# Straight programs, an identity from VectorE and a different row order for m tile 0 in a tuned matmul-subtract kernel

## The chip, the cores and the metric

One core of one Trainium2 chip. The metric is the device time of one execution in microseconds (us), without a profiler; the span that a profile gives is some 2 us shorter (209.0 for a run of 211.0). Where two kernels are compared, they ran in the same rounds on the same chip; a ratio is the mean time of one kernel's fast runs over the mean of the other's of the same rounds, so it is not quite the ratio of the medians that stand beside it.

## The reference

```python
batch, m, k, n = 16, 512, 1024, 768
x         = randn(batch, m, k)   # float32
weight    = randn(k, n)          # float32
sub_value = randn(batch, m, n)   # float32
out       = np.matmul(x, weight) - sub_value      # float32
```

That is 8192 rows, worked on as 64 m tiles of 128 rows. Loads are 62 MB, stores 25 MB.

## The kernel before

Every engine has its own list of instructions, emitted once all lists are complete. SyncE issues 38 large transfers in a fixed order ('x' and 's' are loads, 'o' stores; the numbers are the first m tile and how many):

```python
TRANSFERS = [
    ('x', 0, 1), ('w', 0, 1), ('x', 1, 1), ('w', 1, 1), ('x', 2, 1), ('w', 2, 1),
    ('x', 3, 2), ('w', 3, 1), ('s', 0, 1), ('x', 5, 3), ('s', 1, 3), ('x', 8, 4),
    ('s', 4, 4), ('x', 12, 4), ('s', 8, 8), ('x', 16, 2), ...
    ('x', 24, 8), ('o', 0, 8), ('s', 24, 8), ... ('o', 56, 5), ('o', 61, 2), ('o', 63, 1),
]
```

A run of eight m tiles is a block of 1024 rows in which partition p holds rows 8p to 8p+7, so a transfer of one m tile reads rows that lie eight apart. ScalarE casts x to 16 bits. For most tiles TensorE transposes against an identity matrix that GpSimd makes; for one pair of tiles in three, VectorE transposes (pieces of 32x256 in the trace, 435 ns each). TensorE multiplies, VectorE subtracts. TensorE's program is a straight part and a loop of ten rounds, six tiles each; at the very start it runs matmuls on zeros ("idle") until the first tile is there.

At the start three engines go around their whole program once: in a first turn they branch past it, in a second one they run it.

```python
    turn = nc.alloc_registers("turn", engines=engines)      # PE, DVE, Activation
    nc.regs_mov(turn, 0)
    with nc.body("turn_head", valid_engines=engines):
        nc.br_cmp(turn, 0, on_true="past", on_false="work", comp_op="IS_EQ", engines=engines)
    with nc.body("work", valid_engines=engines):
        act.emit(act.ops)
        dve.emit(dve.ops[:NEAR])          # NEAR = 140
        ...                               # pe: straight part, loop, rest
    with nc.body("past", valid_engines=engines):
        nc.regs_alu(turn, turn, 1, op=mybir.AluOpType.add)
        nc.br_cmp(turn, 2, on_true="turn_head", on_false="rest", comp_op="IS_LT", engines=engines)
    nc.switch_bb("rest")
    dve.emit(dve.ops[NEAR:])
```

## Time and profile before

| | before |
|---|---|
| time, median of 3 runs | 210.98 us (210.87 to 211.11) |
| span of the profile | 209.0 us |
| TensorE busy | 196.5 us, 94% |
| share of the 16 DMA engines' time | 97.7% |
| bytes moved | 87.08 MB |
| first x tile usable | 6.0 us |
| stretch in which TensorE never waits | 45.79 us to its end |
| last output issued, landed | 203.10, 207.75 us |

How to read it: two resources are full at once. The page counts 16 DMA engines for the core. The trace records 16 landings for each of the 38 transfers, one by one, and the first cast starts just after the last of the 16 (6.01 us, the landing at 5.99).

### The profile page before, as it was taken

How to read it: one execution, taken by the hardware profiler on the slowest of the kernel's cores; microseconds unless marked ns; L12 is line 12 of the kernel's file. 1: busy time of each engine (PE TensorE's matmuls, PEld its weight loads, DVE VectorE, ACT ScalarE, POOL GpSimd, SP SyncE). 2: the span in 40 equal slices, each digit the busy share in tenths (PEclk: the TensorE clock that was granted, in tenths of full speed). 3: DMA queues.
4: the chain of work that ended last, by engine and by line, in shares of the span. 5: the costliest groups of instructions: out<-in, count | busy, mean ns of one | idle time of the engine just before them, and what ended most of it. 6: DMA issues, size and time to landing. Idle time of an engine off the chain costs nothing.

```text
span 209.0 us, 2630 instructions
## 1 busy us (share of the span) xinstructions
PE 196.5 (94%) x1234; PEld 75.5 (36%) x700; DVE 127.0 (61%) x216; ACT 109.0 (52%) x113; POOL 1.4 (1%) x9
## 2 busy tenths in 40 slices
PE   6998799979999999999999999999999999999960
PEld 0133334324434433433443443344344244334410
DVE  0132153975994795598299379569839938952330
ACT  2555559615772761945645576193564737507300
POOL 2000000000000000000000000000000000000000
PEclk9999999999999999999999999999999999999996
DMA  6999999999999999999999999999999999999993
GB/s 196 411 429 427 432 424 438 436 415 439 437 439 433 420 423 442 445 426 425 447 426 419 447 419 423 456 439 415 440 436 411 430 437 437 419 433 442 414 411 125
DMA packets 5476, 87.08 MB, mean 417 GB/s; under 512 B 608, under 2 KB 608, under 8 KB 1888
## 3 DMA queue, kind: packets, MB, share of 16 engines
q1 hardware_dynamic: 5472, 87.03, 97.7%
q14 instruction: 3, 0.02, 0.1%
q8 instruction: 1, 0.02, 0.0%
HBM read 61.87 MB, written 25.17 MB: 416 GB/s over the span
## 4 chain that ended last, share of the span: by engine, by line
PE 75%; DMA 12%; DVE 6%; SPq 3%; issue 1%; DVEq 0%
PE po_b L184 67%; DMA so_ring<-in_sub_value_dram 12%; PE pt_b L321 8%; DVE xtp_b L354 3%; DVE so_ring L403 2%; SPq L284 2%; SPq L248 1%; SPq L554 0%; DVEq L60 0%; SPq L134 0%
## 5 line engine op out<-in xcount | busy, mean ns | idle before, releaser
L184 PE MATMUL po_b<-w_sb,xt_b 128*128 128x384 f16 x704 | 126.0, 326 | 0.7 <-DVE w_sb L251 0.7
L403 DVE TENSOR_TENSOR so_ring<-po_b,so_ring 128x768 f32<-128x768 f32 x64 | 60.8, 957 | 58.2 <-PE po_b L184 40.9
L334 ACT COPY xt_b<-pt_b 128x1024 f16<-128x1024 f16 x44 | 44.5, 1012 | 67.2 <-PE pt_b L321 66.3
L354 DVE STREAM_TRANSPOSE xtp_b<-x16p_b 32x256 f32<-32x256 f32 x144 | 62.7, 435 | 2.4 <-ACT x16p_b L303 0.2
L184 PE MATMUL po_b<-w_sb,xtp_b 128*128 128x384 f16 x320 | 61.3, 326 | 1.2 <-DVE xtp_b L354 1.1
L383 PEld LDWEIGHTS <-xt_b 128*128 128x128 f16 x352 | 34.4, 98 | 58.4 <-issue 55.1
L303 ACT CAST x_b<-x_ring 128x1024 f16<-128x1024 f32 x46 | 47.2, 1048 | 4.5 <-DMA x_ring<-in_x_dram 4.5
L321 PE MATMUL pt_b<-ident,x_b 128*128 128x128 f32 x184 | 47.5, 274 | 1.6 <-ACT x_b L303 1.5
L321 PEld LDWEIGHTS pt_b<-ident,x_b 128*128 128x128 f32 x184 | 25.4, 141 | 45.8 <-issue 36.3
L303 ACT CAST x16p_b<-x_ring 128x1024 f16<-128x1024 f32 x18 | 18.8, 1046 | 13.0 <-DMA x_ring<-in_x_dram 13.0
L383 PEld LDWEIGHTS <-xtp_b 128*128 128x128 f16 x160 | 15.7, 98 | 19.8 <-issue 17.7
L251 DVE CAST w_sb<-so_ring 128x768 f16<-128x768 f32 x8 | 4.1, 557 | 15.5 <-DMA so_ring<-in_weight_dram 15.5
L184 PE MATMUL po_b<-idle_x,idle_w 128*128 128x512 f16 x26 | 9.0, 503 | 2.1 <-POOL idle_x L171 2.1
L334 ACT COPY xtp_b<-pt_b 128x1024 f16<-128x1024 f16 x2 | 2.0, 1012 | 2.5 <-PE pt_b L321 2.5
L303 ACT ACT_TABLE_LOAD x1 | 1.3, 1283 | 1.8 <-issue 1.8
L413 PEld LDWEIGHTS <-idle_w 128*128 128x128 f16 x4 | 0.4, 100 | 2.0 <-POOL idle_x L171 2.0
L171 POOL MEMSET idle_x<- 128x512 f16 x1 | 0.5, 530 | 0.0
L485 ACT CAST stub<-ident 128x1 f16<-128x1 f32 x2 | 0.4, 194 | 0.0
L173 POOL TENSOR_SCALAR_AFFINE_SELECT ident<-ident 128x128 f32<-128x128 f32 x1 | 0.3, 294 | 0.1
L462 POOL MEMSET mark<- 128x1 f32 x1 | 0.1, 99 | 24.6 <-ACT xtp_b L334 24.6
L170 POOL MEMSET idle_w<- 128x128 f16 x1 | 0.2, 205 | 0.5 <-SPq L134 0.5
L172 POOL MEMSET ident<- 128x128 f32 x1 | 0.2, 205 | 0.0
(4 smaller groups left out, 0.4 us busy)
## 6 DMA issues: line engine op xcount, KB each, us to landing
so_ring<-in_sub_value_dram SPq DMA_DIRECT2D x7, 3072.0 KB, 24.3
out_dram<-so_ring SPq DMA_DIRECT2D x7, 3072.0 KB, 25.9
x_ring<-in_x_dram SPq DMA_DIRECT2D x5, 4096.0 KB, 22.8
x_ring<-in_x_dram SPq DMA_DIRECT2D x2, 2048.0 KB, 26.5
so_ring<-in_weight_dram SPq DMA_DIRECT2D x4, 768.0 KB, 8.8
x_ring<-in_x_dram SPq DMA_DIRECT2D x1, 3072.0 KB, 28.0
x_ring<-in_x_dram SPq DMA_DIRECT2D x2, 1024.0 KB, 24.4
out_dram<-so_ring SPq DMA_DIRECT2D x1, 1920.0 KB, 10.2
```

What stands on the lines that cost most here:

```text
L171: pool.add(lambda: nc.gpsimd.memset(idle_x, 0.0), then=count("idle"))
L184: return nc.tensor.add_instruction(mybir.InstMatmult(name=nc.get_next_instruction_name(), engine=full.engine, ins=list(full.ins), outs=lis ...
L248: sp.add(lambda st=st, at=at: nc.sync.dma_start(out=st, in_=w_c[at]), then=(sem, 16))
L251: lambda at=at, r=r, st=st: nc.vector.tensor_copy(out=w_sb[:, at, r], in_=st[:, r]),
L284: sp.add(lambda here=here, there=there: nc.sync.dma_start(out=here, in_=there), waits, (sem, 16))
L303: act.add(lambda: nc.scalar.copy(out=to, in_=x_in), waits, count("cast"))
L321: pe.add(lambda: nc.tensor.transpose(words, from_, ident), waits, count("turn") if last else None)
L334: act.add(lambda: nc.scalar.copy(out=to, in_=pt_b[:, b]), waits, count("evac"))
L354: dve.add(lambda: nc.vector.transpose(xt[b * Q : (b + 1) * Q, :, a * Q : (a + 1) * Q], x16[a * Q : (a + 1) * Q, :, b * Q : (b + 1) * Q],), ...
L383: pe.add(lambda weights=weights: nc.tensor.ldweights(weights, tile_position=(0, 0)), [w for w in waits if w[0] in ready])
L403: dve.add(lambda: nc.vector.tensor_tensor(out=o, in0=po[:, :, :NS], in1=o, op=mybir.AluOpType.subtract), [landed["s", mi], (counter["mul"] ...
L413: pe.add(lambda: nc.tensor.ldweights(idle_w, tile_position=(0, 0)), [(counter["idle"], 2)])
```

## The change

Its intent: start the useful work sooner. The jumps at the start hold engines up (TensorE's first matmul starts 0.4 us after its operand is ready) and make them fetch instructions while the first loads run (three fetches, at 2.00 to 3.97 us in the trace of before); a first m tile of 128 consecutive rows reads closer addresses; VectorE is idle at the start and can make the identity as well as GpSimd.

```diff
-S = 8
+SEGMENTS = [(0, 1), (1, 7)] + [(at, 8) for at in range(8, 64, 8)]
...
-    ('x', 24, 8), ('o', 0, 8), ('s', 24, 8), ...
+    ('x', 24, 8), ('o', 0, 1), ('o', 1, 7), ('s', 24, 8), ...
...
+    def view(flat, at, n):
+        first, size = next(one for one in SEGMENTS if one[0] <= at < sum(one))
+        rows = flat[first * P : (first + size) * P].rearrange("(p j) c -> p j c", p=P, j=size)
+        return rows[:, at - first : at - first + n]
...
-    pool.add(lambda: nc.gpsimd.memset(ident, 0.0), then=count("ident"))
-    pool.add(lambda: nc.gpsimd.affine_select(out=ident, in_=ident, ...
+    dve.add(lambda: nc.vector.memset(ones, 1.0), then=count("ident"))
+    dve.add(lambda: nc.vector.memset(ident, 0.0), then=count("ident"))
+    dve.add(lambda: nc.vector.tensor_tensor_scan(out=along, data0=ones, data1=ones, initial=0.0, ...
+    dve.add(lambda: nc.vector.transpose(across, along), ...
+    for a in range(P // Q):
+        here = slice(a * Q, (a + 1) * Q)
+        dve.add(... nc.vector.tensor_tensor(out=ident[here, here], in0=along[here], in1=across[here], op=is_equal) ...
...
-    turn = nc.alloc_registers("turn", engines=engines)
-    ...                                   (the whole block of jumps)
+    for q in (sp, pool, act, dve):
+        q.emit(q.ops)
+    ...                                   (pe: straight part, loop, rest, as before)
```

## The prediction

> **What bounds the kernel now.** I read four views: the page, a table of stretches, the chain of waits, and the timeline of the first microseconds. First the page: the busy tenths of TensorE and DMA in 40 slices, and the DMA queues.
>
> ```profile
> PE   6998799979999999999999999999999999999960
> ...
> DMA  6999999999999999999999999999999999999993
> ...
> q1 hardware_dynamic: 5472, 87.03, 97.7%
> q14 instruction: 3, 0.02, 0.1%
> q8 instruction: 1, 0.02, 0.0%
> ```
>
> The reader is to see two full resources, and a few packets that are not data: instruction fetches. The table of stretches says when each is full (columns: stretch, length, busy time and count on PE, weight load, DVE, ACT, POOL, then clock, DMA share, GB/s):
>
> ```profile
> 2.00:3.00 1.00, 0.95 (x3) 0.10 (x1) 0.00 (x0) 1.00 (x1) 0.12 (x1) 1.00 0.91 168
> 3.00:4.00 1.00, 1.00 (x4) 0.00 (x0) 0.00 (x0) 0.06 (x1) 0.00 (x0) 1.00 1.01 383
> ...
> 6.00:46.00 40.00, 36.43 (x220) 13.03 (x125) 18.38 (x32) 23.59 (x24) 0.10 (x1) 1.00 1.01 426
> 46.00:202.00 156.00, 156.00 (x1008) 62.38 (x575) 107.64 (x183) 84.12 (x88) 0.00 (x0) 1.00 1.00 432
> ```
>
> From 46 to 202 us TensorE never waits, and DMA is full too. So the end is set by when that stretch starts, and by when the slowest DMA engine has drained. What starts the stretch is in the chain of waits (start, length, what):
>
> ```profile
> 8.72 25.85 DMA so_ring<-in_sub_value_dram
> ...
> 34.66 1.82 DVE so_ring L403 x2
> ...
> 45.79 0.81 PE po_b L184 x4
> ```
>
> A sub_value transfer lands at 34.57, VectorE can only then finish tiles 4 and 5, its block transposes come after that, and TensorE waits 1.09 us for them before 45.79. Everything before is loads in queue order. The timeline shows how they pace the start:
>
> ```profile
> 2.05 5.90 PE L184 MATMUL po_b<-idle_x,idle_w 128*128 128x512 f16 x14 [2.05 <-POOL idle_x L171]
> ...
> 6.01 1.05 ACT L303 CAST x_b<-x_ring 128x1024 f16<-128x1024 f32 x1 [2.95 <-DMA x_ring<-in_x_dram]
> ...
> 7.79 0.60 PE L321 MATMUL pt_b<-ident,x_b 128*128 128x128 f32 x4
> 7.90 1.03 DVE L251 CAST w_sb<-so_ring 128x768 f16<-128x768 f32 x2 [7.90 <-DMA so_ring<-in_weight_dram]
> ...
> 11.04 1.03 DVE L251 CAST w_sb<-so_ring 128x768 f16<-128x768 f32 x2 [2.12 <-DMA so_ring<-in_weight_dram]
> ```
>
> The first x tile, issued at 0.94, is usable at 6.0, and each weight piece ends an idle stretch of VectorE. The prediction rests on one closer look at the trace: its sixteen landing records per transfer, one per DMA engine. For the first x tile the median engine lands at 4.49, the 13th at 4.75, the 14th and 15th at 4.81 and 5.26, the last at 5.99. For the first weight piece: median 6.40, 13th 6.63, then 7.15, 7.16, 7.87. At the landing at 34.57: median 33.11, 13th 33.51, then 33.87, 33.89, 34.57. So one engine is 1.46 to 1.50 us behind the median from the first transfer on, and two are 0.77 behind. The lag doesn't shrink while the queue is full; at the last output it is 2.24 (205.50 against 207.75). And every wait ends at the last engine.
>
> Why that engine is late is in the DMA view of the first 6 us:
>
> ```profile
> q1 hardware_dynamic: 282, 1.30, 63.4%
> q14 instruction: 2, 0.02, 2.0%
> q8 instruction: 1, 0.02, 1.0%
> ```
>
> The packet records: an instruction fetch of 8 KB at 2.00 us that took 1651 ns, just as the first x tile starts moving (1.96), then one of 8 KB at 3.97 (309 ns) and one of 16 KB at 3.97 (931 ns). Three engines are late, and three fetches lie there. The fourth fetch of the span is at 162.15 us (8 KB, 324 ns).
>
> [...] three fetches fall within about 2 us after the last jumps (1.64 to 2.04 us in the trace), and only one in the remaining 200. [...] Here rows lie 32 KB apart; in this trace later loads of the same pitch run at 159 ns per 4 KB packet, so a pitch penalty is not shown beyond the first packets (156 to 1101 ns, before 3 us).
>
> **The change part by part.**
>
> 1. The jumps go (TensorE, VectorE, ScalarE). Sequencer time: TensorE starts its idle matmuls at 2.05 though their operand was ready at 1.08+0.53=1.61, so 0.4 us sooner. ScalarE's table load at 1.77 moves to about 1; nothing waits for it. The main effect is the fetches. If none of the three comes before data flows, the last engine should be where the 13th is now: 1.46-0.40 = 1.06 us sooner, on every transfer to 34.57. They may come later[...]; the two that fell in full flow cost their engines 0.77-0.40 = 0.37 us each, less than the cold one, and from different engines they don't add. While TensorE has all it needs that costs nothing.
>
> 2. Does TensorE follow by 1.06? Its 13 idle matmuls run 0.427 us apart, so starting at 1.65 the first transposes begin at about 7.4, not 7.79: only 0.4 gained there, though the cast will be done near 5.9. Then: copy of tile 0 to 9.06, tile 0's first product 9.1; cast of tile 1 8.96 to 10.0, its transposes to 10.5, four idle matmuls to 11.4, second weight piece ready at 12.08-1.06=11.0: it starts at 11.4 instead of 12.13. Tile 1 follows to 13.35, transposes of tile 2 and three idle matmuls to 14.6 (before 15.29), 20 products of 0.163 to 17.85, transposes of tile 3 to 18.3. The last weight piece's casts, done at 19.62 before, are done at 18.56: TensorE is there. So from the fourth weight piece on (19.67 before) it follows the loads fully, about 1.05. The DMA chain to 45.79 moves by the same 1.06, and 156 us of full TensorE carry it to the end: 202.1 becomes about 201.05.
>
> 3. Tile 0 as 128 consecutive rows. Same 512 KB in 4 KB packets. Eight packets of 159 ns per engine are 1.27 us from 1.96; the median completion record goes out near 4.1, so 0.8 to 0.9 us are lost in the cold start. If closeness of rows helps, some comes back: I choose 0.2 of it, range 0 to 0.5. Tiles 1 to 7 get a pitch of 28 KB[...].
>
> 4. One more output DMA (tile 0 apart from 1 to 7): one issue of 0.43 us on a queue whose engine has nothing else to do while data waits ahead of it. Cost 0.
>
> 5. Identity on VectorE: two fills, a short scan, a transpose, four compares. GpSimd's versions took 205 and 294 ns; eight small instructions of at most 0.2 us (estimate from those) end before 3 us. VectorE is free until its first weight piece, at 6.6 at the soonest, and TensorE needs the identity near 7. Hidden.
>
> 6. The end. Today the last output's 16 landings spread from 205.23 to 207.75. Median engines have no gap in their work, so they finish near 205.5 less the 0.2 of point 3; the last one should lag 0.9 (the 13th now: 206.43) to 1.5, giving 206.2 to 206.8 instead of 207.75: 0.95 to 1.55. TensorE's side gives 1.05 plus at most 0.2. Sum: about 1.25 us of 210.98, so 209.7.
>
> **The rivals.** (a) The fetches only move, into the same stretch: with a straight program they may still come in the first microseconds. Then only the 0.2 of point 3 and little else remains: 210.7. [...] Against: the fetch at 162 us shows that some come late. (b) Late fetches stall an engine: the jumps were presumably put there to bring the program in early. A stall of some microseconds on TensorE goes straight to the end, because it has no slack after 46; once gives 211 to 213, in each of the ten rounds of its loop 215 or more. For it: TensorE's program is the longest. Against: between 4 and 162 us there is no fetch while the loop runs, so it stays resident, and removing jumps leaves its size as it is. (c) DMA is the true limit: engines are full to 205 whatever TensorE does, so a sooner TensorE merely waits for x. Then only the drain of the slowest engine counts, and if its late fetches are as costly the gain is 0.3 to 0.7: 210.5. (d) The tile-0 pitch was the whole cold start: up to 0.8 more, 208.9, though TensorE's idle matmuls would eat part.
>
> **Range and chances.** Main path 55%, (a) and (c) together 30%, (b) 6%, (d) 9%. That gives 209.7 as the estimate, 208.8 to 210.9 for 8 in 10. Faster by over 2% needs 4.2 us, more than the start holds: 1%. Slower by over 2% needs a repeated stall: 2%.
>
> **What would show it.** Right: no instruction packets between 2 and 5 us; first x cast near 4.8 to 5.0 instead of 6.01; first weight cast near 6.6 to 6.9 instead of 7.90; first transposes near 7.4; the sub_value landing of 34.57 near 33.3; the steady stretch entered near 44.6; last finish near 201. Wrong: fetches still there by 5 us (a); idle of TensorE after 46 us with no data releaser (b); ScalarE waits on x growing and TensorE waiting for them (c); first cast before 4.6 (d). A first cast over a microsecond sooner with the same end would sink the claim that the early lag reaches the end.

Rival (b)'s stall of some microseconds is supposed, not measured.

## The result, and the profile after

210.76 us median of 4 runs (210.71 to 210.84) against 211.05 (210.87 to 211.21) of before; ratio 0.9990, 95% interval 0.9975 to 1.0004. A repeat (the first experiment) gave 0.9987 (0.9975 to 1.0000). So the change brings some 0.2 to 0.3 us, at the edge of the noise (the intervals reach from 0.5 us to none), where 1.3 were predicted. The predicted time of 209.7 missed by about 1 us; the measured one lies inside the stated range.

The start went as predicted, and further. The timeline of the changed kernel:

```profile
1.67 5.71 PE L198 MATMUL po_b<-idle_x,idle_w 128*128 128x512 f16 x14 [1.67 <-POOL idle_x L178]
...
4.23 1.04 ACT L317 CAST x_b<-x_ring 128x1024 f16<-128x1024 f32 x1 [2.05 <-DMA x_ring<-in_x_dram]
...
6.08 1.03 DVE L265 CAST w_sb<-so_ring 128x768 f16<-128x768 f32 x2 [3.60 <-DMA so_ring<-in_weight_dram]
...
7.21 0.60 PE L335 MATMUL pt_b<-ident,x_b 128*128 128x128 f32 x4
```

The first cast starts at 4.23 instead of 6.01, the first weight cast at 6.08 instead of 7.90, the first transposes at 7.21 instead of 7.79. The DMA view of the first 6 us shows only data, no instruction fetch:

```profile
## 3 DMA queue, kind: packets, MB, share of 16 engines
q1 hardware_dynamic: 338, 1.52, 65.9%
issues: line engine op xcount, KB each, median us to landing
```

The fetches are not gone. The page of the changed kernel counts exactly as many as the page before did:

```profile
q8 instruction: 1, 0.02, 0.0%
q14 instruction: 3, 0.02, 0.0%
```

In its packet records they now start at 35.11 us (16 KB, 931 ns) and at 50.17, 87.23 and 145.07 us (8 KB, 309 ns each). The start and the last wait of TensorE's full stretch, in its timeline:

```profile
44.00 0.81 PE L198 MATMUL po_b<-w_sb,xtp_b 128*128 128x384 f16 x4 [0.88 <-DVE xtp_b L368]
...
50.58 0.81 PE L198 MATMUL po_b<-w_sb,xt_b 128*128 128x384 f16 x4 [0.23 <-ACT xt_b L348]
```

TensorE enters it at 44.00, 1.79 us ahead of before. Then it loses part of that again. The chain of waits of the changed kernel (start, length, what) says to what:

```profile
9.99 38.47 DMA x_ring<-in_x_dram
48.51 0.93 issue
49.44 1.00 ACT xt_b L348
```

A load of x lands at 48.47; on before's chain the load that counted landed at 34.57. From tile 13 on the lead is 1.01 us, from tile 59 on 0.85 (comparing the starts of each tile's first product in the two traces). The last subtraction shows it, before and then after:

```profile
202.11 0.96 DVE L403 TENSOR_TENSOR so_ring<-po_b,so_ring 128x768 f32<-128x768 f32 x1 [1.64 <-PE po_b L184]
```

```profile
201.26 0.96 DVE L417 TENSOR_TENSOR so_ring<-po_b,so_ring 128x768 f32<-128x768 f32 x1 [1.64 <-PE po_b L198]
```

And there the lead ends. The last output, in the DMA view from 202 us on (KB, us from issue to landing), before and then after:

```profile
out_dram<-so_ring SPq DMA_DIRECT2D x1, 384.0 KB, 4.7
```

```profile
out_dram<-so_ring SPq DMA_DIRECT2D x1, 384.0 KB, 5.3
```

It is issued 0.85 us sooner (202.25 instead of 203.10) and takes 0.7 us longer, so it lands at 207.59 instead of 207.75. The landing records say which part of the 16 is late (us; lag is last minus median):

| transfer | before: median, last, lag | after: median, last, lag |
|---|---|---|
| x of tile 0 | 4.49, 5.99, 1.50 | 3.95, 4.21, 0.26 |
| sub_value of tiles 4 to 7 | 33.11, 34.57, 1.46 | 32.38, 32.78, 0.40 |
| x of tiles 12 to 15 | 38.01, 39.46, 1.46 | 37.23, 38.78, 1.55 |
| sub_value of tiles 16 to 23 | 62.40, 63.86, 1.46 | 61.54, 62.97, 1.43 |
| x of tiles 24 to 31 | 72.12, 73.57, 1.45 | 71.78, 74.20, 2.43 |
| last output | 205.50, 207.75, 2.24 | 205.25, 207.59, 2.34 |

Read downward: the changed kernel has no slow DMA engine until 33 us. The 16 KB fetch at 35.1 us makes one, by 1.1 us. At 69.4 us something else adds 1.0, called the event below: sixteen 32 KB packets take 0.25 to 1.56 us longer than the 1.21 us of the others. (Packet records name no engine; by the landings, the slowest one lost most.) At the end the slowest engine is as far behind as it was before.

So the theories. **D**: the end is set by the slowest DMA engine, which has no pause, and not by TensorE. **M**: an instruction fetch is paid by the DMA engine that carries it, whether early or late, so moving it gains nothing at the end. Rivals: **E**, TensorE sets the end and the missing gain is chance; **H**, the event at 69.4 us ate a gain that would have been there; **R**, the early gain comes from the row order and not from the jumps.

### The profile page after: what moved, and what is told of

Same layout as the page of the kernel before. It is cut to its first block, busy times and chain, and to the rows that moved or that the text cites. A ratio compares the mean times of both kernels' runs of the same rounds, so it can differ in the third digit from the quotient of the medians.

```text
span 208.9 us, 2614 instructions
## 1 busy us (share of the span) xinstructions
PE 196.7 (94%) x1234; PEld 75.4 (36%) x700; DVE 127.8 (61%) x224; ACT 108.8 (52%) x113; POOL 1.0 (0%) x7
## 4 chain that ended last, share of the span: by engine, by line
PE 72%; DMA 18%; SPq 4%; ACT 1%; issue 1%; DVE 0%
PE po_b L198 65%; DMA x_ring<-in_x_dram 18%; PE pt_b L335 7%; SPq L298 3%; SPq L262 1%; ACT xt_b L348 0%; DVE so_ring L417 0%; ACT x_b L317 0%; SPq L553 0%; ACT x16p_b L317 0%; SPq L138 0%
## 5 line engine op out<-in xcount | busy, mean ns | idle before, releaser
L187 DVE TENSOR_TENSOR ident<-along,across 32x32 f32<-32x32 f32 x4 | 0.7, 183 | 0.1
```

The costliest lines, as they stand in the source:

```text
L187: dve.add(lambda here=here: nc.vector.tensor_tensor(out=ident[here, here], in0=along[here], in1=across[here], op=mybir.AluOpType.is_equal, ...
```

## The experiments

Times are medians, and each ratio is to before's runs.

### 1. The changed kernel again

No edit.

> The changed kernel once more, for a second trace and a tighter ratio. Theory M (the instruction fetches only move: 16 KB for TensorE at 35.1 us, [...] and the slowest DMA engine carries as much at the end as before): the first x cast again at 4.2, the fetches at the same places within 1 us, the slowest DMA engine 2.0 to 2.5 us behind the median one at the last output, ratio 0.998 to 0.9995. Theory H (the gain was eaten by a chance event, since at 69.4 us all 16 DMA engines took 0.25 to 1.6 us longer for one packet): the event is gone or elsewhere in this trace and the time differs by 0.5 us or more from 210.76.

Measured: 210.70 us, ratio 0.9987 (0.9975 to 1.0000). First x cast at 4.22. Fetches at 29.06, 51.03, 87.39 and 145.25 us: TensorE's came 6 us sooner than in the first trace, outside the 1 us that was expected. It then held up the sub_value load that lands near 33 us (lag 1.83 there instead of 0.40), so TensorE's lead was only 0.47 us. The end lag was 2.64, a little above the expected 2.5. The event was there again, at 69.54. So the event is no accident of one run. Against E this run says nothing: at the end TensorE's lead was 0.38 us smaller than in the first trace, and the traced run, the slowest of its five (211.05), landed its last output 0.34 later too.

### 2. Only the jumps taken away

```diff
-    turn = nc.alloc_registers("turn", engines=engines)
-    ...                                   (the whole block of jumps, from before)
+    for q in (sp, pool, act, dve):
+        q.emit(q.ops)
+    ...                                   (pe: straight part, loop, rest)
```

> Before with the jumps alone taken away: identity on GpSimd and rows of tile 0 as before. Theory M: fetches late as in the changed kernel; the first x cast near 4.6 to 5.0 (6.01 before, 4.23 changed); last output as before within 0.3 us; ratio 0.998 to 1.001. Rival R (the row order made the early gain): the first x cast stays at 5.7 or later.

Measured: 210.68 us, ratio 0.9994 (0.9981 to 1.0007). First x cast at 4.78, against 6.01 before and 4.23 with all three parts. So some 1.2 us of the 1.8 come from the jumps, against R. TensorE kept little of it: its lead was 1.24 at tile 6 but 0.13 from tile 10 on, because its late fetch held up the same sub_value load (landed at 34.44, against 34.57 before). Its fetches lie at 31.05, 57.13, 88.15 and 160.97; no event at 69 us. The last output landed at 207.47, 0.28 before that of before, with a lag of 1.98.

### 3. Only the row order

```diff
-S = 8
+SEGMENTS = [(0, 1), (1, 7)] + [(at, 8) for at in range(8, 64, 8)]
...                                        (view() and ('o', 0, 1), ('o', 1, 7) as in the change; jumps and GpSimd's identity kept)
```

> Before with the new row order alone: jumps and GpSimd identity kept. Theory M: three fetches in the first 5 us, the slowest DMA engine about 1.4 us behind the median from the first transfer on, first x cast 5.5 to 5.9; the median engine lands the first x near 4.0 to 4.2 instead of 4.49; ratio 0.9975 to 1.000. Rival R: first x cast near 4.5.

Measured: 210.72 us, ratio 0.9992 (0.9980 to 1.0004). The median DMA engine landed the first x at 4.12 instead of 4.49, so the row order does help the cold start by 0.4 us. But the first cast came at 6.98, later than before and well outside the 5.5 to 5.9 expected: in this trace the first of the three fetches took 2294 ns instead of 1651, and the slowest engine was 2.83 us behind in the first transfer. TensorE ran 0.98 us behind before all the way. The last output was issued at 204.07, 0.97 later than before, and landed at 207.93, 0.18 later. R falls for good, and a whole microsecond on TensorE moved the end by 0.18.

### 4. TensorE alone jumps

The changed kernel, with the block of jumps put around TensorE's program only.

```diff
+    engines = OrderedEngineSet([mybir.EngineType.PE])
+    ...                                   (the block of jumps, with the pe lines alone)
```

> The changed kernel, with TensorE alone jumping through its program first. Theory M: the 16 KB fetch is again near 4 us instead of 35.1, and costs its DMA engine about 0.4 us early instead of 1.1 at 35; the other fetches stay late; landings up to 33 us are 0.3 to 0.5 later than in the changed kernel, those at 46 to 48 us 0.3 to 0.7 earlier; TensorE's lead over before in its full stretch is 1.2 to 1.5 us instead of 1.01; end 0 to 0.7 us earlier than changed. If the slowest DMA engine at the end is as late as ever, the end stays within 0.2 us of the changed kernel.

Measured: 210.81 us, ratio 0.9997 (0.9984 to 1.0009). The DMA view of its first 6 us:

```profile
q1 hardware_dynamic: 328, 1.47, 65.9%
q8 instruction: 1, 0.02, 1.0%
```

So the 16 KB fetch on queue 8 is TensorE's: it moved with TensorE's jump, to 3.89 us. What it costs was expected wrongly. The first cast came at 5.94, the slowest engine was 1.93 us behind in the first transfer and still 1.55 at 39 us, not 0.4. TensorE's lead was 0.59, not 1.2 to 1.5. The last output landed at 207.73. Early or late, this fetch sets its DMA engine back by 1.1 to 1.6 us; the end is within 0.15 us of the changed kernel's, as the last sentence of the expectation has it.

### 5 and 6. Less to move: before and after

Wrong results: of the last three sub_value loads only the first tile of each eight is loaded, 8.3 MB less.

```diff
+            if kind == "s" and at >= 40:
+                here, there = here[:, :1], there[:, :1]
             sem, value = lane((kind, at))
```

> Before, but of the subtrahend of tiles 40 to 63 only every eighth tile is loaded (8.3 MB of 87 less, wrong results on purpose). Theory D (the end is set by the slowest DMA engine, not by TensorE): DMA is no longer full after some 125 us, TensorE sets the end: last product as before near 202.1, last output issued near 203.1, all 16 landings within 0.6 us of each other, near 205.7; time 208.7 to 209.2, about 2 us less. Theory E (TensorE sets the end in the original too): at most 0.3 us less.

> The changed kernel with the same cut. Theory D: now TensorE's lead of the early part shows in the time: 0.5 to 1.0 us less than the cut kernel before, by as much as its last product is earlier, within 0.2. Theory E: the same difference as between the uncut kernels, 0.3 or less.

Measured: 208.68 us for before with the cut (ratio to before 0.9904, 0.9889 to 0.9919), 207.70 for the changed kernel with it (0.9854, 0.9839 to 0.9868). The stretch from 125 to 202 us has DMA no longer full (the column before the last; GB/s in the last). First before without the cut:

```profile
125.00:202.00 77.00, 77.00 (x497) 30.29 (x281) 50.67 (x85) 38.85 (x42) 0.00 (x0) 1.00 1.00 430
```

Then before and after with it:

```profile
125.00:202.00 77.00, 77.00 (x498) 30.50 (x282) 51.08 (x86) 39.07 (x42) 0.00 (x0) 1.00 0.79 329
```

```profile
125.00:202.00 77.00, 76.17 (x491) 29.92 (x277) 50.67 (x85) 38.18 (x41) 0.00 (x0) 1.00 0.80 334
```

In both the last output then takes only this long from issue to landing, and its 16 landings lie within 0.2 us:

```profile
out_dram<-so_ring SPq DMA_DIRECT2D x1, 384.0 KB, 2.3
```

So a last output that finds the queue free needs 2.3 us; in the uncut kernels it took 4.7 and 5.3. TensorE's end had some 2.4 and 3.0 us to spare there (an estimate from these).

With DMA out of the way the gain is there: 208.68 less 207.70 is 0.98 us, against 0.3 for the uncut kernels. In the profiles the last subtraction starts 1.23 sooner (202.44 and 201.21); that is 0.25 more than the medians show, slightly over the 0.2 allowed, but the two traced runs themselves differ by 1.29 (208.84 and 207.55). So the change does make TensorE earlier by about a microsecond, and in the real kernel the drain of the outputs hides it. E falls.

### 7 and 8. Less for TensorE: before and after

Wrong results: some 9.8 us of matrix work is left out (an estimate: in 60 tiles, two products of 0.163 us move half as much).

```diff
-                    po[:, h, :NS],
+                    po[:, h, : NS // 2 if short and r == 0 else NS],      # short: tile 4 on, c == 2
                     weights,
-                    w_sb[:, c, r, h * NS : (h + 1) * NS],
+                    w_sb[:, c, r, h * NS : h * NS + (NS // 2 if short and r == 0 else NS)],
```

> Before, with some 10 us of TensorE work less: from tile 4 on, one of the eight products of a tile and half moves half its columns (wrong results on purpose). Theory D: TensorE now waits for loads, the time stays within 0.5 us of before, since the slowest DMA engine ends as late as ever. Theory E: 3 to 9 us less.

> The changed kernel with the same cut of TensorE work. Theory D: within 0.5 us of the changed kernel, and the two cut kernels differ by no more than the uncut ones did (0.3). Theory E: 3 to 9 us less.

Measured: 210.82 us (ratio 0.9998, 0.9985 to 1.0011) and 210.83 us (1.0002, 0.9989 to 1.0015), beside 210.83 for before itself in the same rounds. In the traces TensorE's busy time fell by 7.4 us (196.5 to 189.1) and 6.7. That is worth nothing at all. Its waits show where it went (who waits for whom, us in total, times, longest). Before without the cut:

```profile
PE po_b L184 <- DVE xtp_b L354: 1.1, 1, 1.1
...
PE po_b L184 <- DVE so_ring L403: 0.2, 1, 0.2
```

And with it:

```profile
PE po_b L184 <- DVE so_ring L404: 4.0, 3, 3.1
PE po_b L184 <- DVE xtp_b L354: 3.9, 2, 2.2
```

TensorE ran up to 4.5 us ahead of the uncut kernel (at tile 42), ran out of data and waited. The last outputs were issued at 203.30 and 201.52, 1.8 us apart, and landed at 207.72 and 207.67. This is D in its plainest form.

### 9. GpSimd makes the identity again

The changed kernel without its third part: the VectorE lines and the tiles ones, along and across taken out, GpSimd's two lines put back.

> The changed kernel with the identity made on GpSimd again, as before: so the new row order and no jumps, without the third part. What is to be told: whether the event at 69.5 us (all 16 DMA engines 0.3 to 1.6 us slow for one 32 KB packet; there in all five runs that have all three parts, in none of the five others) comes with the identity and its three small tiles, or with rows and straight programs together. If with the identity: no event, the median engine's last landing near 204.8 instead of 205.25, the slowest 1 us sooner than 207.6, time near 210.0. If with the other two: event there, time 210.6 to 210.9.

Measured: 210.88 us, ratio 1.0000 (0.9988 to 1.0012). The event at 69.5 us is gone, as in the first of the two cases named. But the time didn't fall to 210.0: the last landing is 207.78, with a lag of 2.52. The slowest engine was 1.67 behind after TensorE's fetch (29.17 us), 1.92 from 74 us on, 2.33 after 161 us and 2.52 at the end. So H falls: without the event the slack was filled by smaller delays. Of the fourteen traces, the event near 69.5 us is in all eight of kernels with the new row order and VectorE's identity (in one of them TensorE still jumps), and in none of the six others, this one among them. Why three small tiles or eight early VectorE instructions should bring it stays open; no run here separates the two. The packet records show similar stretches elsewhere, and also without VectorE's identity: in experiment 5 at 142 and 150 us, where sixteen and more packets take up to 0.9 and 1.1 us too long. So the identity goes with this one event and not with the kind.

### 10. Which engine is the slow one

The changed kernel with four single-tile loads cut in two.

```diff
+FEWER = {('s', 24): 120, ('s', 25): 112, ('s', 26): 104, ('s', 27): 96}
...
-    ('s', 24, 8),
+    ('s', 24, 1), ('s', 25, 1), ('s', 26, 1), ('s', 27, 1), ('s', 28, 4),
...
+                sp.add(lambda here=here[:cut], there=there[:cut]: nc.sync.dma_start(out=here, in_=there), waits, (sem, 16))
+                sp.add(lambda here=here[cut:], there=there[cut:]: nc.sync.dma_start(out=here, in_=there), [], (sem2, 16))
```

> The changed kernel with four single-tile loads of the subtrahend (tiles 24 to 27, about 79 to 86 us) cut in two, so that the first piece has 120, 112, 104 and 96 partitions. [...] Either way the time stays within 0.6 us of the changed kernel.

Measured: 214.22 us, ratio 1.0160. The cut cost far more than the 0.6 us expected: from 80 to 86 us the DMA engines were full but moved 247 to 261 GB/s, in packets of 3 KB, where the changed kernel moves 404 to 446, mostly in packets of 24 KB. The experiment was to find the slow engine by leaving engines out, one more each time. In the trace the four first pieces have 15, 16, 13 and 16 landings. The late landing was in all four (83.50, 84.89, 86.95 and 88.10, each 1.1 to 1.6 us after the next latest). It was also in the 24 remaining partitions of the third tile, which have 12 landings (87.16, 1.5 after the next). The remaining eight partitions of the first tile had no such landing (82.28 at the latest). So the slow engine seems to have carried a part of each of those five and none of these eight partitions. Which of the sixteen it is was not shown, and no rebalanced version was tried.

### 11 and 12. More fetches

The changed kernel with 512 and 1408 tiny fills of an unused tile at the end of GpSimd's program. Nobody waits for them; they are there to be fetched.

```diff
+    pad = sbuf("pad", [P, 1408], F16)
...
+    for i in range(1408):
+        pool.add(lambda i=i: nc.gpsimd.memset(pad[:, i : i + 1], 0.0))
```

> The changed kernel with 512 tiny fills of an unused tile appended to GpSimd's program (32 KB of instructions, four fetches of 8 KB from about 24 us on; GpSimd has nothing else to do). No engine waits for them. Theory D+M (an instruction fetch is paid by the DMA engine that carries it, and the slowest DMA engine sets the end): each fetch sets one DMA engine back by 0.31 to 0.45 us, 1.2 to 1.8 in all. If that is the engine that is slowest anyway, the time is 1.2 to 1.8 us longer; if it is another one, it stays within its 2.3 us and the time moves by less than 0.3.

> The same with 1408 fills (88 KB, eleven fetches, to about 165 us). Theory D+M: 3.4 to 5 us on one DMA engine: if it is the slowest one, the time is 3.4 to 5 us longer; if another, whose own lag is about 0.3, 1.4 to 3 us longer; the last landing of each transfer falls back step by step at the fetches, and TensorE's waits hardly change before 150 us. Theory E (the end is TensorE's, fetches are hidden): within 0.3 us of the changed kernel.

Measured: with 512, 211.24 us, ratio 1.0002 (0.9987 to 1.0018), so some 0.3 us over the changed kernel's ratio, at the border of the two cases named; lag 2.53 to 2.95 at the last three outputs. With 1408, 217.20 us, ratio 1.0286 (1.0262 to 1.0310): 6.2 us over the changed kernel, from 88 KB of instructions on top of 87 MB. Its page counts them:

```profile
q1 hardware_dynamic: 5616, 87.03, 96.2%
q14 instruction: 14, 0.11, 0.1%
q8 instruction: 1, 0.02, 0.0%
```

Eleven more than the 3 of the changed kernel: 1408/11 = 128 instructions per fetch of 8 KB.

The landings show which engine pays. Up to 39 us the last one is TensorE's fetch, 1.6 to 1.7 behind. Then another engine passes it, and the second-latest stays 1.50 to 1.57 behind (at 54 to 63 us, in both runs). The engine that passes, some 0.3 behind at most at 29 us as all are, is 2.53 behind after four extra fetches (with 512, at 57 us) and 4.36 after seven (with 1408, at 66 us): 0.56 and 0.58 us for each (an estimate, which takes one rank of landings for one engine), against 0.31 us that the packet itself is recorded for. So the extra fetches fell on an engine that had slack, and made it the slowest. At 93 us, after all eleven and the event at 69.5 us, it is 7.08 behind. The median engine didn't lose: 86.38 against 86.40 us in the changed kernel for the sub_value load of tiles 24 to 31.

The time grew by more than the 3.4 to 5 us expected. The slowest engine's landing is 4.6 us later than in the changed kernel at 159 us (158.78 and 154.15) and 6.8 later from 193 us on (199.81 and 192.97); the rest comes in two steps, at 160 to 164 and 184 to 187 us, where the packet records show more stretches like the event. TensorE too waited sooner than expected: it is 5.1 us behind the changed kernel from tile 29 on (105 us), since with a lag that large data comes too late for it. The page's share of DMA time for all these packets is 0.1%. D and M hold: most of the loss, 4.6 of the 6.8 us in this trace, is a cost that is invisible as a share of the total, because it falls on one engine of sixteen. This shows what an added fetch costs; no run takes a fetch away, so what the end would be without the four is not shown.

The runs with all data moved and no extra work for DMA, put together. All columns but the last are of the one traced run; the last is the median of all its runs:

| run | last output issued | median landing | last landing | span of the trace | time |
|---|---|---|---|---|---|
| before | 203.10 | 205.50 | 207.75 | 209.05 | 210.98 |
| changed | 202.25 | 205.25 | 207.59 | 208.88 | 210.76 |
| changed again | 202.63 | 205.30 | 207.93 | 209.23 | 210.70 |
| jumps away only | 202.96 | 205.49 | 207.47 | 208.77 | 210.68 |
| row order only | 204.07 | 206.31 | 207.93 | 209.22 | 210.72 |
| TensorE alone jumps | 202.51 | 205.23 | 207.73 | 209.02 | 210.81 |
| before, less TensorE | 203.30 | 205.79 | 207.72 | 209.02 | 210.82 |
| changed, less TensorE | 201.52 | 205.38 | 207.67 | 208.96 | 210.83 |
| GpSimd's identity | 202.92 | 205.26 | 207.78 | 209.08 | 210.88 |

The issue varies by 2.55 us, the last landing by 0.46. Each span ends 1.3 us after the last landing, whatever the issue was. Why the slowest engine's lag comes out so near to 2 to 2.6 us in kernels whose parts of it differ (a fetch, the event, smaller delays after 160 us) is not settled. No version here beats both kernels by more than noise.

## Why the prediction was wrong, point by point

**What bounds the kernel: half right.** It named two full resources and said that the end is set by the start of TensorE's full stretch and by the drain of the slowest DMA engine. Only the second holds. Before is not bound by TensorE: with 7.4 us less of TensorE's busy time it takes 210.82 us beside 210.83. That TensorE never waits after 46 us doesn't make it the limit.

**Point 1, the fetches leave the start: right, but a term was mis-sized.** No instruction packet between 2 and 5 us, and the lag on the landings to 33 us fell from 1.46 to 0.40, the 1.06 predicted. Landings moved more, by 1.79 at the one of 34.57, because the median moved too. The failing term is "the two that fell in full flow cost their engines 0.77-0.40 = 0.37 us each, less than the cold one". The prediction had matched lags to fetches by guess: the largest lag to the cold 8 KB fetch. Experiment 4 brings back TensorE's 16 KB fetch alone, and the first transfer's lag is 1.93. That fetch costs 1.1 to 1.6 us wherever it lies, and it moved to 29 to 35 us, where it took 0.8 to 1.4 us of TensorE's lead (1.79 to 1.01 in one trace, 1.84 to 0.47 in the other).

**"While TensorE has all it needs that costs nothing": the step that failed.** It prices a late fetch by TensorE's waits. The fetch is work for a DMA engine for which the landings show no pause until 207 us, so it is paid at the end whenever it comes: with TensorE's fetch at 3.89 us the last lag was 2.49, with the fetch at 35.11 and 29.06 it was 2.34 and 2.64. After the 8 KB fetches at 50 and 145 us an engine was some 0.4 and 1.0 us further behind too (the second-latest landing of the changed kernel). Experiments 11 and 12 show the price of an added fetch. The prediction named this outcome itself: the first cast came 1.78 us sooner with the same end, which was to sink the claim that the early lag reaches the end.

**Point 2, TensorE follows by 1.06: close, and beside the point.** First transposes 7.21 (7.4 predicted), full stretch at 44.00 (44.6), last subtraction at 201.26 (201). The lead was real: 0.98 us of time in the pair with less to move. That it came out so near is in part luck: TensorE gained 1.79 and lost some of it to its late fetch, and in the second trace the lead at the end was 0.47, with the jumps alone taken away 0.13.

**Point 3, consecutive rows: right within its range.** With rows alone the median first landing went from 4.49 to 4.12, 0.37 where 0.2 was chosen. The slowest 4 KB packet of before took 1101 ns, that of the changed kernel 487; the median is 159 in both.

**Points 4 and 5: right in time.** The extra store and VectorE's identity show no cost in the end; experiment 9 differs from the changed kernel's ratio by 0.001, within the intervals. The event that goes with the identity was foreseen by nobody.

**Point 6, the end: wrong by the size of one lag.** "The last one should lag 0.9 to 1.5": it lagged 2.34. Of that, 1.15 came with TensorE's fetch at 35 us and 1.0 with the event. In before the lag had grown too, from 1.47 at 154 us to 2.24 at the end, which the prediction left out. The median landed at 205.25, 205.3 having been predicted; that is luck in part, since the median engine was 0.86 ahead at 62 us (61.54 and 62.40) and 0.34 at 72, after the event (71.78 and 72.12). The whole error of 1 us is in the lag.

**The rivals.** Rival (c), DMA is the true limit and only the drain counts, was the right one, with a gain of 0.3 to 0.7 us named for it; 0.2 to 0.3 was measured. Its sign came too: ScalarE's waits for x grew from 17.5 us to 21.1 in the pages. It got too small a chance because the full PE row looked like a limit. Rival (a) had the fetches stay in the first microseconds; they came at 29 us and later. Rival (b) didn't happen: TensorE's waits after 46 us in the changed kernel are for data (those without a releaser are 0.2 us in the whole trace), and its loop runs at the pace of before. Rival (d)'s sign, a first cast before 4.6 us, did come (4.23), but rival (d) is ruled out by experiment 2: with the old rows the first cast still came at 4.78.

## What to carry to other kernels

When the DMA engines are full to the end, look at the landings of one transfer engine by engine: here the time was the slowest engine's, and delays of a microsecond on one of sixteen didn't show in any mean share. To learn which of two full resources is the limit, take work away from each in turn and time it; a resource that never waits may still have no say (here 7.4 us less of TensorE's busy time left 210.82 us beside 210.83). Moving a cost from a busy start to a busy middle gained nothing here, because the same unit paid for it and had no pause (TensorE's fetch at 3.89 or at 35.11 us: last landing at 207.73 and 207.59).
